# A gated ConvFFN on one core: from six token windows with copied leading columns to five windows of 512 and 384 columns with a carry table

## The chip, the core and the metric

The kernel runs on one core of a Trainium2 chip. The metric is the device time of one execution in microseconds (us), the median of several runs. The engines are TensorE (PE, matmul, with PEld for its weight loads), VectorE (DVE), ScalarE (ACT), GpSimd (POOL) and SyncE (SP, which here only issues transfers).

## The reference

One layer of a hybrid encoder over a prompt of 2048 tokens and 128 sample tokens (8 streams of 16), D_MODEL 1024: a mixer (a Mamba-2 group and a forgetting-attention group side by side), an output projection with a residual add, then the gated ConvFFN (D_FF 2816, convolution width 3) with a residual add, then a last RMSNorm. The change touches the FFN alone:

```python
def rmsnorm(x, g):
    y = xf * lax.rsqrt(jnp.mean(xf * xf, axis=-1, keepdims=True) + EPS)
    return y * g
def causal_dwconv(x, prev, w, b):          # w has 3 taps
    xp = jnp.concatenate([prev, x], axis=1)
    y = b
    for j in range(w.shape[0]):
        y = y + xp[:, j:j + L] * w[j]
    return y, xp[:, L:]
def conv_ffn(n, prev, w_up, cw, cb, w_down):
    u, new = causal_dwconv(n @ w_up, prev, cw, cb)
    g, v = u[..., :D_FF], u[..., D_FF:]
    return (silu(g) * v) @ w_down, new
# in the layer: x = h + conv_ffn(rmsnorm(h, norm2_g), ...); at the end rmsnorm(x, final_norm_g)
```

## The kernel before, in words

The 2176 tokens are 17 tiles of 128 rows, the sample tokens being the last tile. Everything up to the output projection writes h, a row of 1024 per token, to memory (`h_d`). The FFN then goes over the tokens in three parts (`FPARTS`); a part holds two windows of columns. All 198 weight blocks are read again for each part.

- **The weights.** `load_w` reads a block of 128x1024 on ACT's queue into one of 3 `raw` buffers; ACT casts it to a high half (L102) and POOL subtracts for the low half (L105, `split`), into one of 6 `wr` buffers. Every product is formed of three matmuls: high by high, high by low, low by high (L113 to L115, `mm3`).
- **The rows of a window.** `prep` makes `nT`, the normalised rows transposed: it loads a tile of h, ACT squares and sums it, POOL makes the inverse root (`rsq`, L108 and L109), DVE multiplies (L925), PE transposes eight blocks (`tp`, L929), ACT copies the high half and DVE subtracts the low one. In the parts after the first it loads the tile into the buffer `y`, which afterwards collects the result. A window's `nT` carries PAD2 = 2 leading columns, copied from the end of the window before it (L906), so that the convolution has its two preceding tokens: 386 columns for three tiles, and 258 for the last window (one prompt tile, the sample tile, the 2 columns).
- **Up.** For each of 22 feature blocks f (`NFF`) `up` makes a gate row block and a value row block: 24 matmuls each into one PSUM bank (`mm`, 5 banks), then ACT's eviction with the last tap and the bias (L951), DVE's two other taps, each reading the bank (L953), for the sample tile four more small ones and an add (L957, L959) and copies of the last columns to the output table `cs2` (L960, L961); then ACT's SiLU (L963), DVE's product of gate and value (L964) and its split into `ht` (L104, L105).
- **Down.** Two blocks f make a group (`GRP` = 2), eleven groups a part. `down` adds for each tile and each half of 512 columns six matmuls into one bank (`dn`, 3 banks; L975 to L977), which DVE adds to `y` (L978). With 6 tiles that is 72 matmuls a group, with 5 tiles 60.
- **Order.** A framework's scheduler places the instructions on the engines; PE's order is fixed by it, and a buffer that is not free makes the engine wait. Within a part a group's `down` matmuls stand among the next group's first up matmuls. At a change of part the first window of the next part is prepared after the last group's ups, and the second one in the first group of the next part. After the last group `finish` normalises each tile of `y` and writes it (L984 to L989).

## Time and profile before

| | |
|---|---|
| runs | 3183.7, 3184.08, 3178.56 us; median 3183.7 us |
| the profiled execution | 3180.02 us by its own time, of which the trace spans 3178.3 us; mean granted TensorE clock 0.978 |
| FFN in the trace | from the first up matmul at 1576.06 us to the last down matmul, which starts at 3170.47 us |
| busy in the span | PE 95%, DVE 58%, ACT 32%, POOL 28% |

Times in the trace are counted from the start of the span. A busy matmul in it overlaps the next one, so what one matmul costs in a stream is read from the distance of two starts, not from its duration.

### The profile page before, as it was taken

To read this page: it belongs to the slowest core of one execution; us is meant where nothing else is said; L and a number is where in the kernel's file an instruction comes from. 1 tells how busy PE (TensorE), PEld (TensorE's weight loads), DVE (VectorE), ACT (ScalarE), POOL (GpSimd) and SP (SyncE) were. 2 spreads that over 40 slices of the span, in tenths; PEclk is the share of its full clock that TensorE was granted. 3 is DMA by queue.
4 is the path that set the end of the run, shared out by engine and by line. 5 is a ranking of instruction groups with operands and counts; after the bars stand their busy time and mean duration, and the time that the engine had idled before them with its cause. 6 is when DMAs were issued, how large, how long until landed. Compare 5 with 4: busy or idle time off the path is not lost.

```text
span 3178.3 us, 45508 instructions
## 1 busy us (share of the span) xinstructions
PE 3035.1 (95%) x17808; PEld 2671.8 (84%) x17808; DVE 1829.3 (58%) x3325; ACT 1024.1 (32%) x1778; POOL 882.4 (28%) x574
## 2 busy tenths in 40 slices
PE   5998988899999998999999999999999999999999
PEld 5886866788778875677899999989999999999998
DVE  5355465757574655552355555566555556766666
ACT  3343332434333433322322222233222223322222
POOL 3223311332232223100232232323232232433332
PEclk9998988999999998999999999999999999999999
DMA  4856864576547545543621221233122222322221
GB/s 161 256 180 197 246 200 128 165 215 178 148 152 211 157 137 178 169 144 111 234 79 58 64 67 54 67 100 100 53 74 60 67 66 71 109 74 80 68 71 67
DMA packets 233854, 398.36 MB, mean 125 GB/s; under 512 B 62624, under 2 KB 118568, under 8 KB 233640
## 3 DMA queue, kind: packets, MB, share of 16 engines
q1 hardware_dynamic: 180072, 234.22, 23.9%
q10 hardware_dynamic: 53568, 161.24, 16.2%
q8 instruction: 140, 2.29, 0.3%
q14 instruction: 74, 0.61, 0.1%
HBM read 317.13 MB, written 78.25 MB: 124 GB/s over the span
## 4 chain that ended last, share of the span: by engine, by line
PE 84%; DMA 7%; DVE 4%; issue 2%; SPq 1%; POOL 1%; ACT 1%; ACTq 0%; POOLq 0%; DVEq 0%
PE mm L113 11%; PE mm L114 11%; PE mm L115 11%; PE pv L662 6%; PE dn L975 5%; PE dn L976 5%; PE dn L977 5%; PE mm L413 3%; PE mm L414 3%; PE mm L415 3%; PE dn L873 2%; PE mm L366 2%; PE dn L875 2%; PE mm L367 2%; PE dn L874 2%; PE mm L368 2%
## 5 line engine op out<-in xcount | busy, mean ns | idle before, releaser
L105 POOL TENSOR_TENSOR wr<-raw,wr 128x1024 fp32r<-128x1024 f32 x198 | 475.9, 2411 | 1032.8 <-ACT wr L102 985.8
L113 PE MATMUL mm<-nT,wr 128*128 128x386 f32 (+1 forms) x2112 | 696.5, 330 | 1.3 <-ACT wr L102 0.8
L114 PE MATMUL mm<-nT,wr 128*128 128x386 f32 (+1 forms) x2112 | 695.3, 329 | 0.1
L115 PE MATMUL mm<-nT,wr 128*128 128x386 f32 (+1 forms) x2112 | 694.5, 329 | 0.0
L953 DVE SCALAR_TENSOR_TENSOR ac<-mm,cw,ac 128x384 f32<-128x384 f32 (+1 forms) x528 | 301.7, 572 | 345.0 <-ACT ac L951 337.3
L951 ACT ACTIVATE ac<-mm,cw 128x384 f32<-128x384 f32 (+1 forms) x264 | 172.5, 653 | 785.9 <-PE mm L115 782.0
L978 DVE TENSOR_TENSOR y<-y,dn 128x512 f32<-128x512 f32 x374 | 255.3, 684 | 267.3 <-PE dn L977 264.5
L114 PEld LDWEIGHTS mm<-nT,wr 128*128 128x128 f32 x2112 | 399.4, 189 | 6.8 <-DVE nT L105 0.3
L113 PEld LDWEIGHTS mm<-nT,wr 128*128 128x128 f32 x2112 | 397.6, 188 | 7.7 <-ACT wr L102 1.1
L115 PEld LDWEIGHTS mm<-nT,wr 128*128 128x128 f32 x2112 | 398.0, 188 | 5.7
L105 POOL TENSOR_TENSOR cmw<-craw,cmw 128x1024 fp32r<-128x1024 f32 (+1 forms) x96 | 231.1, 2411 | 380.4 <-ACT cmw L102 295.9
L413 PE MATMUL mm<-nT,cmw 128*128 128x256 f32 (+2 forms) x1024 | 309.2, 302 | 1.6 <-DVE g_2k L300 1.6
L637 DVE TENSOR_REDUCE nm<-s 128x1 f32<-128x512 f32 (+2 forms) x320 | 192.5, 606 | 190.2 <-PE s L634 109.4
L414 PE MATMUL mm<-nT,cmw 128*128 128x256 f32 (+2 forms) x1024 | 298.6, 292 | 0.0
L415 PE MATMUL mm<-nT,cmw 128*128 128x256 f32 (+2 forms) x1024 | 297.9, 291 | 0.0
L662 PE MATMUL pv<-pr,v 128*128 128x512 f32 (+3 forms) x640 | 295.6, 552 | 2.2 <-POOL v L602 1.8
L975 PE MATMUL dn<-wr,ht 128*128 128x512 f32 x748 | 294.4, 394 | 2.8 <-DVE y L978 1.7
L976 PE MATMUL dn<-wr,ht 128*128 128x512 f32 x748 | 292.8, 391 | 0.0
L977 PE MATMUL dn<-wr,ht 128*128 128x512 f32 x748 | 290.1, 391 | 0.0
L102 ACT CAST wr<-raw 128x1024 fp32r<-128x1024 f32 x198 | 203.2, 1042 | 173.7 <-PE dn L977 161.5
L697 ACT ACTIVATE pr<-s 128x512 f32<-128x512 f32 (+1 forms) x320 | 169.7, 531 | 269.7 <-PE s L693 182.9
L634 PE MATMUL s<-ks,q 68*128 68x512 f32 (+2 forms) x320 | 201.4, 635 | 10.8 <-DMA q<-q_d 7.0
(287 smaller groups left out, 5194.9 us busy)
## 6 DMA issues: line engine op xcount, KB each, us to landing
raw<-in_w_up ACTq DMA_DIRECT2D x132, 512.0 KB
raw<-in_w_down ACTq DMA_DIRECT2D x66, 512.0 KB
craw<-in_w_cm ACTq DMA_DIRECT2D x64, 512.0 KB
k<-k_d SPq DMA_DIRECT2D x80, 256.0 KB
craw<-in_w_tm ACTq DMA_DIRECT2D x24, 512.0 KB
q_d<-qk SPq DMA_DIRECT2D x96, 128.0 KB
k_d<-qk SPq DMA_DIRECT2D x96, 128.0 KB
ks<-k_d SPq DMA_DIRECT2D x80, 136.0 KB
```

What stands on the lines that cost most here:

```text
L105: leng.tensor_sub(lo, src, hi.bitcast(F32))
L113: T.matmul(ps[:, :W], whi(k), wt[:, 0, k, :W], start=k == 0, stop=False)
L114: T.matmul(ps[:, :W], whi(k), wt[:, 1, k, :W], start=False, stop=False)
L115: T.matmul(ps[:, :W], wlo(k), wt[:, 0, k, :W], start=False, stop=k == n - 1)
L413: T.matmul(ps[:, :W], wc[:, 0, k, :], wk[:, 0], start=k == 0, stop=False)
L414: T.matmul(ps[:, :W], wc[:, 0, k, :], wk[:, 1], start=False, stop=False)
L415: T.matmul(ps[:, :W], wc[:, 1, k, :], wk[:, 0], start=False, stop=k == KT - 1)
L662: m = T.matmul(pv[:, of:512], vr[:, jj], pr[:, :512 - of], start=first, stop=last)
L953: V.scalar_tensor_tensor(ac[:, 0:n], ps[:, j:j + n], cw2[:, ct, j:j + 1], ac[:, 0:n], op0=ALU.mult, op1=ALU.add)
L975: T.matmul(ps, ht[:, 0, ts_], wd[:, 0, cc], start=x == 0, stop=False)
L976: T.matmul(ps, ht[:, 0, ts_], wd[:, 1, cc], start=False, stop=False)
L977: T.matmul(ps, ht[:, 1, ts_], wd[:, 0, cc], start=False, stop=x == len(g) - 1)
```

## The change

The windows become 512, then 256 and the sample tile (384 columns), 512, 384, 384; the parts have 7, 7 and 3 tiles, and the last part has a single window. The leading columns go. Instead `up` keeps the last two prompt columns of every row block in a table `cry` (a copy by DVE for each row block and window, into `cs2` in the last window), and in the four windows that do not begin at token 0 DVE adds each of the two earlier taps in two instructions: the inner columns from the PSUM bank, and the first two or the first column from `cry`. Both inputs of that second instruction lie in SBUF. Line numbers of the kernel after are one to ten lower; its taps are L943, the taps from the table L945, the copies L946, product L956, split L103 and L104, transposes L917, and down L967 to L970.

`prep` no longer shares `y`: it loads h into a buffer `nt` of its own (2 of them), squares in two halves, and `load_y` loads the `y` tiles after the first ups of each part. The two windows have an `nT` buffer each. The first window of the next part is prepared in the last group between the ups of its first and second window, the second one ahead of that group's `down`. `ht` has 3 buffers of 7 tiles, before 4 of 5 or 6. `finish` squares in halves.

```diff
-PAD2 = 2
 FPARTS = [
-    [(0, 384, False), (384, 768, False)],
-    [(768, 1152, False), (1152, 1536, False)],
-    [(1536, 1920, False), (1920, 2048, True)],
+    [(0, 512, False), (512, 768, True)],
+    [(768, 1280, False), (1280, 1664, False)],
+    [(1664, 2048, False)],
 ]
...
+    def load_y(c):
+        ys_[c] = yp.tile([P, D], F32, tag="y", name="y")
+        dA(ys_[c], h_d[c])
+
+    def prep(w, e):
+        W = win_width(w, 0)
+        wt = nTp.tile([P, 2, KT, (512, 384)[e]], F32R, tag=f"nT{e}", name="nT")
         for c in win_tiles(w):
...
-                src = yp.tile([P, D], F32, tag="y", name="y")
-                dA(src, h_d[c])
-                ys_[c] = src
-                S.activation(nt, src, AF.Square, accum_out=ss[:, 0:1])
+            dA(nt, h_d[c])
+            for a in range(2):
+                jk = tp.tile([P, 512], F32, tag="ac0", name="ac")
+                S.activation(jk, nt[:, a * 512:(a + 1) * 512], AF.Square, accum_out=ss[:, a:a + 1])
+            V.tensor_add(ss[:, 0:1], ss[:, 0:1], ss[:, 1:2])
             rsq(ss[:, 0:1], D)
...
             for j in range(2):
-                V.scalar_tensor_tensor(ac[:, 0:n], ps[:, j:j + n], cw2[:, ct, j:j + 1], ac[:, 0:n], op0=ALU.mult, op1=ALU.add)
+                d = 2 - j
+                wj = cw2[:, ct, j:j + 1]
+                V.scalar_tensor_tensor(ac[:, d:n], ps[:, 0:n - d], wj, ac[:, d:n], op0=ALU.mult, op1=ALU.add)
+                if w[0]:
+                    V.scalar_tensor_tensor(ac[:, 0:d], cry[:, ct, j:2], wj, ac[:, 0:d], op0=ALU.mult, op1=ALU.add)
+            V.tensor_copy((cs2 if w[1] == SEQ else cry)[:, ct, 0:2], ps[:, n - 2:n])
...
-                hts[f] = bp3.tile([P, 2, len(tiles) * P], F32R, tag="ht", name="ht", bufs=4)
+                hts[f] = bp3.tile([P, 2, 7 * P], F32R, tag="ht", name="ht", bufs=3)
...
-                if f0 == 0 and x > 0:
-                    prep(part[1])
-                    wins.append(nwin[-1])
-                for f in fs:
-                    one_up(f, 1)
+                if end and nxt:
+                    new.append(prep(nxt[0], 0))
+                if nw > 1:
+                    for f in fs:
+                        one_up(f, 1)
...
-            if f0 + GRP >= NFF and not last:
-                prep(FPARTS[x + 1][0])
+            if end and len(nxt) > 1:
+                new.append(prep(nxt[1], 1))
             down(g, tiles)
...
-    nTp = F.enter_context(tc.tile_pool(name="nT2", bufs=2, side="right", reuse_waits="tile"))
+    nTp = F.enter_context(tc.tile_pool(name="nT2", bufs=1, side="right", reuse_waits="tile"))
```

How the order on the engines changes is shown at three places. In the rows a name such as `ac_26725` is one buffer of the tile `ac`. First, DVE in the last part before: one block f of its 384-column window.

```order
L953 SCALAR_TENSOR_TENSOR ac_25736<-mm_25711,cw2_15371,ac_25736 128x384 x2
L953 SCALAR_TENSOR_TENSOR ac_25765<-mm_25740,cw2_15371,ac_25765 128x384 x2
L964 TENSOR_TENSOR ac_25736<-ac_25736,ac_25765 128x384
L104 CAST ht_25700<-ac_25736 128x384
L105 TENSOR_TENSOR ht_25700<-ac_25736,ht_25700 128x384
```

DVE in the last part of the kernel after: one block f of its only window, up to the cast.

```order
L943 SCALAR_TENSOR_TENSOR ac_26725<-mm_26700,cw2_15391,ac_26725 128x382
L945 SCALAR_TENSOR_TENSOR ac_26725<-cry_15402,cw2_15391,ac_26725 128x2
L943 SCALAR_TENSOR_TENSOR ac_26725<-mm_26700,cw2_15391,ac_26725 128x383
L945 SCALAR_TENSOR_TENSOR ac_26725<-cry_15402,cw2_15391,ac_26725 128x1
L946 COPY cs2_15401<-mm_26700 128x2
L943 SCALAR_TENSOR_TENSOR ac_26757<-mm_26732,cw2_15391,ac_26757 128x382
L945 SCALAR_TENSOR_TENSOR ac_26757<-cry_15402,cw2_15391,ac_26757 128x2
L943 SCALAR_TENSOR_TENSOR ac_26757<-mm_26732,cw2_15391,ac_26757 128x383
L945 SCALAR_TENSOR_TENSOR ac_26757<-cry_15402,cw2_15391,ac_26757 128x1
L946 COPY cs2_15401<-mm_26732 128x2
L956 TENSOR_TENSOR ac_26725<-ac_26725,ac_26757 128x384
L103 CAST ht_26689<-ac_26725 128x384
```

The two taps of a row block stood back to back, each in one instruction; now each is followed by one that reads the table, and a copy comes behind, also before the product of the two row blocks.

Second, PE in the last group of the first part, where the first rows of the next part are transposed. Before, they come behind the last up matmul of the group:

```order
L114 MATMUL mm_19402<-nT_15166,wr_19246 128x386
L115 MATMUL mm_19402<-nT_15166,wr_19246 128x386
L929 MATMUL tp_19455<-ident_71,nt_19447 128x128 x4
L929 MATMUL tp_19462<-ident_71,nt_19447 128x128 x4
L929 MATMUL tp_19477<-ident_71,nt_19469 128x128 x4
L929 MATMUL tp_19484<-ident_71,nt_19469 128x128 x4
L975 MATMUL dn_19513<-wr_19437,ht_19165 128x512
L976 MATMUL dn_19513<-wr_19437,ht_19165 128x512
```

After, they come behind the last up matmul of the first window and nine down matmuls of the first block f (`ht_19671`); the second window's ups (not shown) follow later.

```order
L967 MATMUL dn_20176<-wr_20076,ht_19671 128x512
L968 MATMUL dn_20176<-wr_20076,ht_19671 128x512
L969 MATMUL dn_20176<-wr_20076,ht_19671 128x512
L917 MATMUL tp_19833<-ident_71,nt_19822 128x128 x4
L917 MATMUL tp_19840<-ident_71,nt_19822 128x128 x4
L917 MATMUL tp_19858<-ident_71,nt_19847 128x128 x4
L917 MATMUL tp_19865<-ident_71,nt_19847 128x128 x4
L967 MATMUL dn_20160<-wr_20081,ht_19746 128x512
L968 MATMUL dn_20160<-wr_20081,ht_19746 128x512
...
L969 MATMUL dn_20176<-wr_20081,ht_19746 128x512
L917 MATMUL tp_19883<-ident_71,nt_19872 128x128 x4
```

Before, the first down matmuls of both blocks read tiles of the first window, whose rows of `ht` were made while the second window's ups ran. Now the down matmuls of the second block (`ht_19746`) read rows of the window that has just ended; they stand right behind the transposes of two tiles, and the third tile's transposes stand nine of them later.

Third, DVE at that place, before:

```order
L953 SCALAR_TENSOR_TENSOR ac_19398<-mm_19373,cw2_15371,ac_19398 128x384 x2
L953 SCALAR_TENSOR_TENSOR ac_19427<-mm_19402,cw2_15371,ac_19427 128x384 x2
L964 TENSOR_TENSOR ac_19398<-ac_19398,ac_19427 128x384
L105 TENSOR_TENSOR nT_19445<-tp_19455,nT_19445 128x4x128
L105 TENSOR_TENSOR nT_19445<-tp_19462,nT_19445 128x4x128
L104 CAST ht_19238<-ac_19398 128x384
L978 TENSOR_TENSOR y_15539<-y_15539,dn_19513 128x512
L105 TENSOR_TENSOR nT_19445<-tp_19477,nT_19445 128x4x128
L105 TENSOR_TENSOR ht_19238<-ac_19398,ht_19238 128x384
```

And after:

```order
L943 SCALAR_TENSOR_TENSOR ac_19812<-mm_19787,cw2_15391,ac_19812 128x510
L943 SCALAR_TENSOR_TENSOR ac_19812<-mm_19787,cw2_15391,ac_19812 128x511
L946 COPY cry_15402<-mm_19787 128x2
L104 TENSOR_TENSOR nT_19821<-tp_19833,nT_19821 128x4x128
L956 TENSOR_TENSOR ac_19782<-ac_19782,ac_19812 128x512
L104 TENSOR_TENSOR nT_19821<-tp_19840,nT_19821 128x4x128
L104 TENSOR_TENSOR nT_19821<-tp_19858,nT_19821 128x4x128
L104 TENSOR_TENSOR nT_19821<-tp_19865,nT_19821 128x4x128
L103 CAST ht_19746<-ac_19782 128x512
L104 TENSOR_TENSOR ht_19746<-ac_19782,ht_19746 128x512
```

The product and split for the last value row block made in that window were divided by two subtractions for `nT`; now by four, and the cast that the down matmuls of `ht_19746` read stands behind all four.

## Rows read from the trace of the kernel before

**Rows 1.** the page: busy time, share and instructions of each engine

```profile
PE 3035.1 (95%) x17808; PEld 2671.8 (84%) x17808; DVE 1829.3 (58%) x3325; ACT 1024.1 (32%) x1778; POOL 882.4 (28%) x574
```

**Rows 2.** busy time by stretch: a group of part 0, then of part 2

```profile
core 0: us, PE busy (x) PEld busy (x) DVE busy (x) ACT busy (x) POOL busy (x), PEclk, DMA share, GB/s
1687.73:1738.24 50.51, 50.51 (x266) 47.49 (x265) 27.93 (x41) 13.22 (x18) 14.35 (x8) 1.00 0.20 63
2842.48:2884.76 42.28, 42.28 (x255) 39.82 (x254) 28.13 (x59) 12.48 (x18) 14.63 (x8) 1.00 0.25 75
```

**Rows 3.** timeline of PE (start us, us, engine line op): three widths

```profile
1849.80 0.34 PE L113 MATMUL mm<-nT,wr 128*128 128x386 f32 x1
...
1859.70 0.34 PE L115 MATMUL mm<-nT,wr 128*128 128x386 f32 x1
...
2128.19 0.40 PE L975 MATMUL dn<-wr,ht 128*128 128x512 f32 x1
...
2130.02 0.39 PE L977 MATMUL dn<-wr,ht 128*128 128x512 f32 x1
...
2813.12 0.28 PE L113 MATMUL mm<-nT,wr 128*128 128x258 f32 x1
...
2815.88 0.29 PE L115 MATMUL mm<-nT,wr 128*128 128x258 f32 x1
```

**Rows 4.** groups by line and form, 1576:3179 (busy us, mean ns | idle before)

```profile
L105 POOL TENSOR_TENSOR wr<-raw,wr 128x1024 fp32r<-128x1024 f32 x198 | 475.9, 2411 | 1032.8 <-ACT wr L102 985.8 <-issue 38.9 <-PE dn L976 4.4
...
L953 DVE SCALAR_TENSOR_TENSOR ac<-mm,cw,ac 128x384 f32<-128x384 f32 x440 | 271.1, 617 | 337.4 <-ACT ac L951 331.2
L978 DVE TENSOR_TENSOR y<-y,dn 128x512 f32<-128x512 f32 x374 | 255.3, 684 | 267.3 <-PE dn L977 264.5
...
L964 DVE TENSOR_TENSOR ac<-ac 128x384 f32<-128x384 f32 x110 | 173.4, 1577 | 3.7
L951 ACT ACTIVATE ac<-mm,cw 128x384 f32<-128x384 f32 x220 | 147.7, 671 | 706.4 <-PE mm L115 702.5 <-POOL wr L105 3.7
...
L105 DVE TENSOR_TENSOR ht<-ac,ht 128x384 fp32r<-128x384 f32 x110 | 63.2, 574 | 3.0
...
L959 DVE TENSOR_TENSOR ac<-ac,sc 128x16 f32<-128x16 f32 x44 | 51.7, 1176 | 0.0
L104 DVE CAST ht<-ac 128x384 fp32r<-128x384 f32 x110 | 39.3, 357 | 2.9
...
L929 PE MATMUL tp<-ident,nt 128*128 128x128 f32 x88 | 11.2, 273 | 1.8 <-DVE nt L925 1.8
...
L960 DVE COPY cs<-mm 128x2 f32<-128x2 f32 x44 | 6.6, 149 | 0.0
```

**Rows 5.** busy time by stretch: the two changes of part (columns as above)

```profile
2091.84:2253.75 161.91, 158.12 (x842) 147.12 (x841) 104.70 (x153) 58.36 (x90) 53.43 (x43) 1.00 0.32 98
2657.85:2800.21 142.36, 140.94 (x815) 131.22 (x814) 102.61 (x184) 52.74 (x82) 50.52 (x37) 1.00 0.30 97
```

**Rows 6.** waits of PE in 1576:3179 (us in total, times, longest)

```profile
PE tp L929 <- DVE nt L925: 1.8, 3, 1.3
```

**Rows 7.** timeline of SP's queue, ACT and DVE around one early tile

```profile
1553.00 0.37 SPq L913 DMA_DIRECT2D nt<-h_d  x1
...
1557.46 0.63 ACT L916 ACTIVATE ac<-nt 128x512 f32<-128x512 f32 x1 [2.52 <-DMA nt<-h_d]
...
1560.89 1.28 DVE L925 SCALAR_TENSOR_TENSOR nt<-nt,ss,g2B 128x1024 f32<-128x1024 f32 x1 [0.71 <-POOL ss L109]
```

**Rows 8.** timeline of DVE and POOL in part 2

```profile
2806.45 2.40 POOL L105 TENSOR_TENSOR wr<-raw,wr 128x1024 fp32r<-128x1024 f32 x1 [0.23 <-ACT wr L102]
...
2807.59 1.30 DVE L959 TENSOR_TENSOR ac<-ac,sc 128x16 f32<-128x16 f32 x1
```

**Rows 9.** timeline of PE: an idle time ahead of the FFN

```profile
402.38 0.77 PE L634 MATMUL s<-ks,q 68*128 68x512 f32 x1 [4.29 <-DMA q<-q_d]
```

**Rows 10.** busy time by stretch around that idle time

```profile
402.00:408.00 6.00, 5.62 (x27) 3.08 (x28) 2.46 (x8) 0.54 (x3) 0.00 (x0) 0.50 0.42 149
```

70 lines of the change are left out of this document (28 added, 42 removed).

## The prediction

> **What bounds the kernel now.** The page's line of engines comes first: PE is busy 95% of the span, DVE 58% [rows 1]. The FFN is tighter still. One group of part 0, taken as a stretch, is 50.51 us long and PE is busy in all of it; one of part 2 is 42.28 us and again full, at a granted clock of 1.00, while DVE works 27.93 and 28.13 us and POOL 14.35 and 14.63 [rows 2]. So in the body of a part the time is PE's matmuls and nothing else. What one costs is read in the timeline from start to start [rows 3]: 386 columns 9.90 us over 56 steps, 176.8 ns; 258 columns 2.76 over 23, 120.0 ns; 512 columns (down) 1.83 over 8, 228.8 ns. Check: 192 x 0.1768 + 72 x 0.2288 = 50.4 us, the group's 50.51; 96 x (0.1768 + 0.1200) + 60 x 0.2288 = 42.2 us, the other's 42.28.
>
> Only at the changes of part does PE lose time. The stretch 2091.84 to 2253.75 is three groups plus 48 transposes; 88 of them are 11.2 us of busy time, 0.127 each [rows 4], and since busy time counts the overlap too I take 0.11 from start to start, an estimate: 161.91 - 3 x 50.51 - 5.3 = 5.1 us lost. The other holds one group of 50.51, two of 42.28 and 40 transposes: 142.36 - 135.07 - 4.4 = 2.9 us [rows 2, 5]. Together 8.0 us. The waits that PE shows by name are small: for the transposes three, 1.8 us in all [rows 6].
>
> **The change part by part**, against the profiled execution's own 3180.0 us.
>
> *Up matmuls: -22 us.* A window takes 24 matmuls for each of 44 row blocks (22 f, gate and value), 1056. Before, one matmul of each of the six windows is 5 x 176.8 + 120.0 = 1004.0 ns; after there are two of 512 and three of 384. For 384 I take the 386 row less two columns at (176.8 - 120.0)/128 = 0.444 ns: 175.9. For 512 there is a down row of equal width, 228.8; a row in up form is not in the trace. After: 457.6 + 527.7 = 985.3, saving 18.7 x 1.056 = 19.8 us. The period of whole groups gives more: with 228 for 512 the 386 come to 177.6 and 258 to 120.3, saving 23.4. I take 22. Bounds: the straight line through 386 and 258 gives 232.7 for 512, saving 11.5 us; 384 columns at the slope alone, without any fixed price, 170.5, would save 37. The down matmuls, 2244, do not change, nor the 198 weight blocks, nor the 136 transposes.
>
> *Changes of part: +6 us (-3 to +12).* At the first one three waits are new, from the order shown. (1) The down matmuls of `ht_19746` need the cast of a row block whose last matmul ends at t = 0. Nine downs (2.06 us) and 16 transposes (1.76) cover 3.8 us. The chain is ACT's eviction (0.67 at 384 columns, so about 0.8 at 512), two taps at 0.617 x 512/384 = 0.82, a copy, one subtraction for `nT` that starts at about 3.1 us, after the first transposes and ACT's copy of them (all subtractions and the product of 512 elements at 0.574 x 512/384 = 0.77), the product, three more subtractions, the cast (0.48): 3.1 + 5 x 0.77 + 0.48 = 7.4 us [rows 4]. PE waits 3.6 us. (2) Only two `nt` buffers exist, so the third tile's load starts when the first tile's transposes end, at 2.9 us. From a load's issue to the end of DVE's multiplication one early tile took 1553.00 to 1562.17 = 9.2 us [rows 7]: ready at 12.1, while PE, after wait (1) and nine downs, is there at 9.5: 2.6 us more. (3) The last tile of the second window has 12 + 9 downs and 8 transposes ahead, 5.7 us against 9.2: 3.5 us. The second change of part has (1) with 384 columns, about 2, and (3) shortened by it, 1.5. Sum 13.2 (3.6 + 2.6 + 3.5 + 2 + 1.5); I add 1 us for the clock. An idle PE costs more than its wait: after 4.29 us of idle time earlier in the kernel the granted clock was 0.50, so 1.2 instead of 2.4 GHz, for 6 us [rows 9, 10], some 3 us of work. What a wait of 3 us does to it no row shows; between nothing and these 3 us I take a third. 14.2 against the 8.0 lost before. Lower bound: if loads land early enough, (2) and (3) vanish and 5 us are left, -3. Upper: waits half longer and one stretch at half clock, +12.
>
> *DVE in the last part: +6.5 us (0 to +16, at the extreme +35).* A group there is 96 x 0.176 + 36 x 0.2288 = 25.1 us of PE, and one window a group leaves DVE fewer matmuls to hide behind. DVE needs 8 taps at 0.617, 4 copies and 8 table taps at 0.149 (no row has a table tap; it lies between the two-column copy, 0.149, and the 128x16 add, 1.176, whose inputs both lie in SBUF, and I count the excess below), two products and two subtractions at 0.574, two casts at 0.357, six adds at 0.684: 4.9 + 1.8 + 2.3 + 0.7 + 4.1 = 13.8 us [rows 4]. That fits. But an operation with both inputs in SBUF waits for POOL here: the product at 384 columns has a mean of 1577 ns where the subtraction of the same shape has 574, and the 128x16 add 1176 [rows 4]; in the timeline that add starts while POOL subtracts and takes 1.30 us [rows 8]. In a group of part 2 this costs DVE 2 x 1.0 + 4 x 1.03 = 6.1 us of POOL's 14.6, 42%. In the last part ten operations a group are of that kind, and POOL does its 6 x 2.41 = 14.5 us in 25.1. At 42% DVE is at 19.9 us, at 100% at 28.3, above PE's 25.1: +3.2 x 11 = +35. The value taken is nearer the first: a product or a table tap can be held by each POOL instruction only once. What is left is latency: the last up of a group has 9 downs and 29 matmuls, 7.2 us, until PE needs its rows of `ht`; the chain is 0.67 + 1.23 + 0.45 + 0.57 + 0.36 = 3.3 us alone, and with one or two holds of POOL (2.4 each) and two adds ahead (1.4) 7.1 to 9.5. About 0.6 us a group, 11 groups.
>
> The Trainium skill (SBUF — State Buffer, Who interferes with whom) says that a DVE instruction with two SBUF inputs contends with a GpSimd instruction that reads SBUF, and that the second to issue is blocked, not slowed. The trace agrees, by the 1577 and 1176 ns.
>
> *The same table taps in parts 0 and 1: +1 (0 to +5).* There DVE has 58 us a group (192 matmuls of 0.202 on average, 84 of 0.2288) for work of 33 to 47 us (its 27.93 a group of 6 tiles and two windows, scaled to 7, and all of POOL's 14.35 on top); only the changes of part feel it.
>
> *The end: +1.5.* Behind the last up matmul nine downs (2.06 us) stand ahead of those that read its `ht`, ready 3.3 to 3.9 us later: +1.8. Squares in halves give back 0.3.
>
> *Edits at nothing.* The copies of leading columns, the squares by halves and the wider `y` loads hide beside 50 us of matmuls a group; if the loads of `y` were late, their first use is 38 us after the first ups, far more than 9.2. Three `ht` buffers instead of four: the one that is reused has been read by `down` two row blocks earlier; if not, each group waits for a chain of about 3.5 us. Weights are read as often, but in the last part in 25.1 us a group instead of 42.28, which takes the DMA share of 0.25 [rows 2] to about 0.42; POOL's halves stay ahead by six `wr` buffers; without that a group loses up to 2.4 us.
>
> Sum: -22 + 6 + 6.5 + 1 + 1.5 = -7: 3173.0 of the execution's own time. The median of the runs is 3.7 us above the profiled one and the fastest run 1.5 below it; I forecast 3174.
>
> **The rivals.**
>
> *Full gain.* The scheduler's waits are covered: loads land before they are needed, POOL and DVE miss each other. For it: DVE's share in the last part is about 80% at the 42% above. Against it: the order, where nine downs stand against a chain of 9.2 us. -22 - 3 + 0 + 1 + 1.5 = -22.5, so 3158.5.
>
> *No change.* Waits at the changes of part and in the last part eat the gain: +12, +10, +1 and +1.5 against -22, +2.5 or 3183.5. Or up matmuls follow the straight line of the two up widths (11.5 saved instead of 22): 3184.5 with the other terms as above. For it: both up widths are in the trace and 512 in up form is not; against it, both group periods come out with 228.8 for a down matmul of that width.
>
> The Trainium skill (TensorE: Matmul & The Clock Gate, Back-to-back issue gap) gives columns/2.4 + 2.5 ns for a matmul alone, so hardly a fixed price. By it the change would save only 7.9 us and the sum would be about 3188; the same section calls it too high at 512 in a stream, where it has 131 ns, and the trace shows neither: 176.8 for 386 columns against 163.3, 228.8 for 512.
>
> *Slower.* DVE becomes the bound in the last part: table taps behind POOL hold DVE, `ht` comes late, and each group of 25.1 us grows. It decides from 1.5 us a group beyond my 0.6 (16 us over eleven groups, to 3190); with all of POOL's time it is +35 instead of +6.5, 3202.5; I put it at 3196. For it: ten operations of the kind that [rows 8] shows and POOL at 58%; against it: at 42% DVE has 5 us spare in each group.
>
> **How the numbers follow.** Chances: forecast (3166 to 3181) 0.48, full gain 0.12, no change (by waits, 0.13, by the line, 0.10) 0.23, slower 0.17. The measurement tells 0.2%, 6.4 us, from no change: faster below 3177.3, slower above 3190.1. The forecast lies below for three quarters (0.36, the full gain adds 0.12, and 0.06 of the no-change cases fall below): 0.54; slower 0.17; the same 0.29. The range reaches down to the full gain and up to the start of the slower case, leaving out half of the one and most of the other: 3158 to 3192; the likeliest one's own is 3166 to 3181.
>
> **What would show it.** In the profile after: up at 512 from start to start 228 and at 384 about 176; PE full in the groups of the first two parts, in 58.1 us; groups of 25 to 26 us in the last part; waits of PE named tp behind L913 and dn behind the cast L103 at two places, 13 us together; L945 with a mean above 0.5 us. Wrong would be: 512 at 232 or more, groups of the last part above 27.5 us, or changes of part that lose less than 6 or more than 20 us.

## The result and the profile after

The kernel after takes 3195.54 us (median of 7 runs, 3186.15 to 3196.97), the kernel before 3178.56 us in the runs beside it (7 runs, 3176.26 to 3184.08): a ratio of 1.0045, 95% interval 1.0031 to 1.0058. The change makes the kernel slower, by about 14 us by that ratio (17 between the medians); the forecast was 3174, its range 3158 to 3192.

The profiled execution of after is one of 3195.54 us, with a span of 3193.8 us, 15.5 more than before. The first up matmul starts at 1580.37 us instead of 1576.06. Of these 4.3 us, 3.6 are there at the last matmul of attention's value product (1501.59 instead of 1498.03 us), ahead of the change. From that matmul to the first up it is 78.0 us before and 78.8 in every other kernel profiled here, while the first up itself starts anywhere between 1568 and 1583 us: what comes ahead of the value product differs from one profiled execution to the next, whatever the edit. So the comparison goes from the first up matmul to the end of the last down matmul, 1594.6 us before and 1604.6 after, and stretch by stretch.

First the groups, as stretches of after (the columns are those of [rows 2]): one of the first part, one of the last, and the stretch behind a long wait, of which more below.

```profile
core 0: us, PE busy (x) PEld busy (x) DVE busy (x) ACT busy (x) POOL busy (x), PEclk, DMA share, GB/s
1747.39:1805.78 58.39, 58.39 (x278) 50.68 (x276) 39.63 (x75) 13.49 (x18) 14.59 (x7) 1.00 0.16 54
3000.84:3025.93 25.09, 25.09 (x133) 23.62 (x132) 22.71 (x32) 9.36 (x13) 15.04 (x6) 1.00 0.36 126
2200.00:2211.00 11.00, 8.94 (x34) 7.47 (x35) 7.89 (x13) 5.03 (x12) 2.45 (x4) 0.69 0.38 123
```

PE is full in both kinds of group, as in [rows 2], although DVE is busy for 22.71 of 25.09 us in the last part. Eleven groups of each part make 11 x (58.38 + 58.37 + 25.09) = 1560.2 us, against 11 x (50.51 + 50.51 + 42.27) = 1576.2 before: 16 us less. What a matmul costs is again read from start to start, in the timeline of PE of after:

```profile
1773.58 0.34 PE L112 MATMUL mm<-nT,wr 128*128 128x384 f32 x1
...
1781.85 0.34 PE L114 MATMUL mm<-nT,wr 128*128 128x384 f32 x1
1782.03 0.40 PE L112 MATMUL mm<-nT,wr 128*128 128x512 f32 x1
...
1786.69 0.40 PE L114 MATMUL mm<-nT,wr 128*128 128x512 f32 x1
```

384 columns take 8.27 us over 47 steps, 176.0 ns, and 512 columns 4.66 over 20, 233 ns.

Between the groups PE waits more than before. Its waits in the FFN of after, which answer to [rows 6]:

```profile
PE dn L967 <- DVE ht L103: 8.4, 4, 2.8
PE dn L967 <- DVE y L970: 5.4, 5, 1.4
PE tp L917 <- DVE nt L913: 4.2, 3, 2.4
PE mm L114 <- POOL wr L104: 2.4, 3, 1.6
PE tp L917 <- DVE ss L911: 2.1, 1, 2.1
...
```

To place this, the FFN is cut into stretches, and the loss of a stretch is its length less its matmuls at their price in a full group (up 177.6 ns for 386 columns, 120.3 for 258, 233.0 for 512, 176.0 for 384, down 227.8, a transpose 109). These prices are fitted to the groups' lengths, with one price for a down matmul in all kernels; [rows 3] have 176.8 for 386 columns and 228.8 for a down. "Start" goes to the third group, a change from the first up of a part's last group to the fourth group of the next part, "end" from the last group to the last down matmul; the stretches between lose at most 0.6 us in any kernel here. In the first change of after, for example, all of the loss lies ahead of the next part's second group: 2156.14 to 2297.14 is 141.0 us and holds 192 ups of 512, 192 of 384, 168 downs and 56 transposes, 122.9 us; 18.1 are lost. The last column is the time from there to the end of the span.

| us | FFN | start | first change | second change | end | behind it |
|---|---|---|---|---|---|---|
| before | 1594.6 | 0.9 | 5.2 | 2.8 | 0.0 | 7.6 |
| after | 1604.6 | 6.9 | 18.1 | 8.1 | 2.2 | 8.9 |

So 16 us are gained and 26 lost again: 6.0 at the start, 12.9 and 5.3 at the changes, 2.2 at the end. With 4.3 ahead of the FFN and 1.3 behind it this is the 15.5 us of the spans, to within the rounding and the few tenths of the stretches between.

At the first change the rows of after show each wait that the prediction named. PE, and the clock behind it:

```profile
2200.34 0.57 PE L967 MATMUL dn<-wr,ht 128*128 128x512 f32 x1 [2.82 <-DVE ht L103]
2200.70 0.63 PE L968 MATMUL dn<-wr,ht 128*128 128x512 f32 x1
2201.13 0.63 PE L967 MATMUL dn<-wr,ht 128*128 128x512 f32 x1
...
2205.04 1.07 PE L917 MATMUL tp<-ident,nt 128*128 128x128 f32 x8 [0.79 <-DVE nt L913]
...
2232.79 1.07 PE L917 MATMUL tp<-ident,nt 128*128 128x128 f32 x8 [2.11 <-DVE ss L911]
2236.63 0.50 PE L967 MATMUL dn<-wr,ht 128*128 128x512 f32 x1 [1.38 <-DVE y L970]
...
2245.15 1.94 PE L917 MATMUL tp<-ident,nt 128*128 128x128 f32 x8 [2.44 <-DVE nt L913]
```

After the 2.82 us of waiting for the cast the down matmuls follow at 0.43 us instead of 0.23: the granted clock of that stretch is 0.69 (above). It is 0.56 from 2200.3 to 2203 and from 2207 to 2210.6 us, and 0.87 between the two, where PE waits twice more. The wait at 2232.79 and the one at 2236.63 were not foreseen. The second one has its cause in these rows of DVE and POOL at that place:

```profile
2233.23 0.47 DVE L943 SCALAR_TENSOR_TENSOR ac<-mm,cw,ac 128x254 f32<-128x254 f32 x1
2233.62 2.36 DVE L945 SCALAR_TENSOR_TENSOR ac<-cry,cw,ac 128x2 f32<-128x2 f32 x1
2235.90 0.67 DVE L970 TENSOR_TENSOR y<-y,dn 128x512 f32<-128x512 f32 x1
```

```profile
2233.59 2.37 POOL L104 TENSOR_TENSOR wr<-raw,wr 128x1024 fp32r<-128x1024 f32 x1
```

A table tap of two columns stands on DVE for as long as POOL subtracts, and the add to y behind it, which frees a PSUM bank for the next down matmul, comes some 2.1 us late (the same tap takes 0.21 us where POOL is idle). Over the FFN of after the groups by form say how often:

```profile
L945 DVE SCALAR_TENSOR_TENSOR ac<-cry,cw,ac 128x1 f32<-128x1 f32 x176 | 222.6, 1265 | 0.0
...
L945 DVE SCALAR_TENSOR_TENSOR ac<-cry,cw,ac 128x2 f32<-128x2 f32 x176 | 91.7, 521 | 0.0
...
L104 DVE TENSOR_TENSOR ht<-ac,ht 128x384 fp32r<-128x384 f32 x66 | 51.7, 783 | 1.8
...
L103 DVE CAST ht<-ac 128x384 fp32r<-128x384 f32 x66 | 40.3, 610 | 1.8
L956 DVE TENSOR_TENSOR ac<-ac 128x384 f32<-128x384 f32 x66 | 38.5, 583 | 0.8
```

The 352 taps hold DVE for 314 us. The product of 384 columns, held to 1577 ns in [rows 4], now takes 583 (the one of 512 columns 1039): the taps ahead of it take its place behind POOL. The cast and the subtraction that follow have become longer (357 to 610, 574 to 783). In the trace, 204 of the 352 taps overlap no subtraction of POOL, and they take 0.20 to 0.22 us; the 148 that do overlap one take 1.83 on average.

At the second change PE waits for the cast of ht twice, 1.89 and 2.37 us. Ahead of the second of these casts, finish's two products stand on DVE beside two subtractions, and a tap of two columns follows that is held for 2.30 us more:

```profile
2914.19 5.65 DVE L983 SCALAR_TENSOR_TENSOR y<-y,ss,gfB 128x512 f32<-128x512 f32 x2
...
2920.56 2.30 DVE L945 SCALAR_TENSOR_TENSOR ac<-cry,cw,ac 128x2 f32<-128x2 f32 x1
```

```profile
2914.09 5.21 POOL L104 TENSOR_TENSOR wr<-raw,wr 128x1024 fp32r<-128x1024 f32 x2
```

At the start, two rows of after: SP issues nine loads of y in a row, and the cast of a weight block waits 9.34 us for transfers.

```profile
1583.90 5.57 SPq L897 DMA_DIRECT2D y<-h_d  x9
...
1590.96 1.05 ACT L101 CAST wr<-raw 128x1024 fp32r<-128x1024 f32 x1 [9.34 <-DMA y<-h_d]
```

Before, SP issued the nine loads of y between 1507 and 1515 us, ahead of the last output projections:

```profile
1507.21 1.14 SPq L1017 DMA_DIRECT2D y<-h_d  x2
...
1509.85 2.18 SPq L1017 DMA_DIRECT2D y<-h_d  x4
1512.90 1.95 SPq L921 DMA_DIRECT2D y<-h_d  x3
```

The change opens the pool of y only when the output projection's buffers are given back.

### The profile page after: what moved, and what is told of

It reads as the page before. It is cut to its first block, busy times and chain, and to the rows that moved or that the text cites. A ratio compares the mean times of both kernels' runs of the same rounds, so it can differ in the third digit from the quotient of the medians.

```text
span 3193.8 us, 43834 instructions
## 1 busy us (share of the span) xinstructions
PE 3024.8 (95%) x16752; PEld 2566.9 (80%) x16752; DVE 2013.4 (63%) x3721; ACT 1004.8 (31%) x1768; POOL 891.5 (28%) x574
## 5 line engine op out<-in xcount | busy, mean ns | idle before, releaser
L104 POOL TENSOR_TENSOR wr<-raw,wr 128x1024 fp32r<-128x1024 f32 x198 | 485.7, 2461 | 1029.2 <-ACT wr L101 993.7
L114 PE MATMUL mm<-nT,wr 128*128 128x384 f32 (+1 forms) x1760 | 635.6, 361 | 2.4 <-POOL wr L104 2.4
L112 PE MATMUL mm<-nT,wr 128*128 128x384 f32 (+1 forms) x1760 | 635.9, 361 | 0.3 <-ACT wr L101 0.3
L113 PE MATMUL mm<-nT,wr 128*128 128x384 f32 (+1 forms) x1760 | 635.0, 361 | 0.0
L970 DVE TENSOR_TENSOR y<-y,dn 128x512 f32<-128x512 f32 x374 | 252.5, 682 | 246.0 <-PE dn L969 245.8
L943 DVE SCALAR_TENSOR_TENSOR ac<-mm,cw,ac 128x511 f32<-128x511 f32 (+5 forms) x440 | 281.9, 641 | 190.8 <-ACT ac L938 183.8
L114 PEld LDWEIGHTS mm<-nT,wr 128*128 128x128 f32 x1760 | 331.0, 188 | 35.7 <-POOL wr L104 3.6
L112 PEld LDWEIGHTS mm<-nT,wr 128*128 128x128 f32 x1760 | 331.3, 188 | 33.9 <-ACT wr L101 0.7
L113 PEld LDWEIGHTS mm<-nT,wr 128*128 128x128 f32 x1760 | 331.2, 188 | 32.8
L938 ACT ACTIVATE ac<-mm,cw 128x512 f32<-128x512 f32 (+1 forms) x220 | 156.0, 710 | 604.8 <-PE mm L114 545.0
L104 POOL TENSOR_TENSOR cmw<-craw,cmw 128x1024 fp32r<-128x1024 f32 (+1 forms) x96 | 231.1, 2411 | 379.4 <-ACT cmw L101 300.8
L945 DVE SCALAR_TENSOR_TENSOR ac<-cry,cw,ac 128x2 f32<-128x2 f32 x352 | 314.3, 893 | 0.0
L967 PE MATMUL dn<-wr,ht 128*128 128x512 f32 x748 | 295.3, 395 | 13.8 <-DVE ht L103 8.4
L101 ACT CAST wr<-raw 128x1024 fp32r<-128x1024 f32 x198 | 203.3, 1042 | 194.6 <-PE dn L969 176.0
```

What stands on the lines that cost most here:

```text
L104: leng.tensor_sub(lo, src, hi.bitcast(F32))
L112: T.matmul(ps[:, :W], whi(k), wt[:, 0, k, :W], start=k == 0, stop=False)
L113: T.matmul(ps[:, :W], whi(k), wt[:, 1, k, :W], start=False, stop=False)
L114: T.matmul(ps[:, :W], wlo(k), wt[:, 0, k, :W], start=False, stop=k == n - 1)
L945: V.scalar_tensor_tensor(ac[:, 0:d], cry[:, ct, j:2], wj, ac[:, 0:d], op0=ALU.mult, op1=ALU.add)
L967: T.matmul(ps, ht[:, 0, ts_], wd[:, 0, cc], start=x == 0, stop=False)
```

## The experiments

Theory: 26 us are lost at the start and at the changes of part, by (a) a burst of y loads ahead of weight loads, (b) two `nt` buffers that make transposes late, (c) table taps that POOL holds where DVE's queue is what PE waits for; and the gain of the matmuls is smaller than forecast since 512 columns cost 233 ns in an up matmul. Rival: DVE, held by POOL, slows the groups throughout. All readings are of one profiled execution each, in the stretches above; the ratio to the kernel before, measured beside it on the same chip, stands with them. How far the two can be trusted is seen from e5_pitch, which does the work of after: start, first and second change lose 5.5, 19.0 and 8.3 us there against 6.9, 18.1 and 8.1, yet its ratio is 1.0018 against 1.0045, and in its trace the last value product comes 8 us earlier. So the ratios of two kernels differ here by 0.3% with no cause in the FFN, and none of the single edits e1 to e4 and e8 has a ratio below e5's. What an edit is worth is read from the stretches, and there a difference of 1 us shows nothing.

**The y loads held back** (e1_ygate; 7 y buffers, since the two that are free would load for the next part).

```diff
-YB = 9
+YB = 7
...
+        if ht is not None:
+            V.tensor_copy(ys_[c][:, 0:2], ht[:, 0, 0:2].bitcast(F32))
         dA(ys_[c], h_d[c])
...
-                            load_y(c)
+                            load_y(c, hts[fs[n // 4]] if x == 0 else None)
```

> The kernel after, with 7 instead of 9 y buffers, and the y loads of the first part held back by a two-column copy out of ht (the first four tiles until the first block's ht is there, the other three until the second's). Theory A, that the 6.9 us lost in the first two groups of part 0 (0.9 before) come from weight loads queued behind a burst of nine y loads: the wait of the weight cast at 1591 us and PE's waits there go, the loss of the first two groups falls from 6.9 to 1 to 2 us, FFN from first up to last down from 1604.3 to about 1599 us, the rest of the stretches unchanged. Rival B, that the wider matmuls need the first weights sooner: the loss stays at 5 to 7 us, FFN about 1604.

Start 2.4, first change 16.8, second 10.0, end 2.2, FFN 1600.6; ratio 1.0028 (1.0013 to 1.0042). The wait of 9.34 us is gone (the weight cast there waits 3.3 for its load), theory (a) holds for 4.5 of the 6 us. The second change got 1.9 us worse without an edit there; where POOL's subtractions fall beside DVE can have shifted, but that is not shown.

**Four nt buffers** (e2_nt4; the third and fourth tile of a window from another pool, the squares into a tile of their own, 7 y buffers).

```diff
-            nt = tp.tile([P, D], F32, tag="nt", name="nt")
...
+            tq = more[0] if more and n % 4 > 1 else tp
+            nt = tq.tile([P, D], F32, tag="nt", name="nt")
...
-                jk = tp.tile([P, 512], F32, tag="ac0", name="ac")
+                jk = more[0].tile([P, 512], F32, tag="jk", name="jk", bufs=1) if more else tp.tile([P, 512], F32, tag="ac0", name="ac")
```

> The kernel after, with 7 y buffers, two more nt buffers for the third and fourth tile of a window, and a tile of its own for the unused squares, which stood in ac0. Theory A, that the two nt buffers (and the squares that wait for ac0) make the transposes late at the changes of part: the waits of PE on nt and ss there (6.3 us in 4) go, the loss at the first change falls from 18.1 to about 9 us, at the second from 8.2 to about 6; FFN about 1594 us (with two y loads fewer at the start another 1 to 2 less). Rival B, DVE's queue is what is late there (nt multiplications behind held table taps): the waits only change their name, the loss stays above 14, FFN above 1600.

Start 8.7, first change 11.1, second 10.5, FFN 1602.0; ratio 1.0021 (1.0009 to 1.0032). The waits for transposes shrink (one of 2.0 us is left), 7 us are won at the first change, but the downs there now wait 4.6 us for y, and the second change is worse. At the start PE waits 3.6 us at once for POOL: with free buffers the scheduler squares the next part's first tiles there, and POOL makes their roots ahead of the first weights. Neither theory fits whole; (b) is a part.

**Without the table taps** (e3_notap; the first columns of four windows lack their earlier taps).

```diff
-                if w[0]:
-                    V.scalar_tensor_tensor(ac[:, 0:d], cry[:, ct, j:2], wj, ac[:, 0:d], op0=ALU.mult, op1=ALU.add)
```

> The kernel after without the 352 table taps (L945): the first two columns of four windows lack their earlier taps; the copies into the table stay. Theory A, that the taps cost time only at the changes of part, where DVE's queue is late anyway: groups stay at 58.4 and 25.1 us, the loss at the first change falls by 2 to 4 us (two of its waits on y stand behind taps held 2.3 us by POOL), FFN about 1600 us. Rival B, that DVE held by POOL is the cause of the slower kernel: FFN falls by 10 us or more, to 1594 or less.

Start 5.4, first change 15.2, second 7.8, FFN 1600.6; ratio 1.0025 (1.0014 to 1.0036). The groups are 58.4 to 58.5 and 25.1 us long, no shorter than with the taps. So 314 us of DVE time cost 4 us, all outside the full groups; the rival, that DVE held by POOL slows the groups throughout, falls. What the held taps cost at the changes isn't settled by this run: PE's waits there only change (for the cast of ht 4.1 instead of 2.8 us at the first change, for y 1.1 instead of 2.5).

**The preparations at their old places** (e4_prepback).

```diff
-                if end and nxt:
-                    new.append(prep(nxt[0], 0))
+                if f0 == 0 and x > 0 and nw > 1:
+                    wins.append(prep(part[1], 1))
...
-            if end and len(nxt) > 1:
-                new.append(prep(nxt[1], 1))
+            if end and nxt:
+                new.append(prep(nxt[0], 0))
```

> The kernel after with the preparations at their old places: the first window of the next part behind the last group's ups of both windows, the second window in the first group of the next part. Theory A, that the new place puts the cast for the second block's down matmuls behind four subtractions for nT and the third tile's load behind nine downs: the wait on the cast (2.9 us and the half clock behind it) goes, the loss at the first change falls from 18.1 to 8 to 10 us and at the second from 8.2 to 4 to 6; FFN about 1592 us. Rival B, the two nt buffers alone cause the loss wherever the preparation stands: the loss at the first change stays above 13, FFN above 1598.

First change 12.7, second 9.6, FFN 1600.3; ratio 1.0024 (1.0011 to 1.0037). The place is worth 5 us at the first change, 1.5 of which the second gives back, and it doesn't remove the loss: one wait for the cast of ht, now of 3.7 us, stands elsewhere. The run doesn't decide between its two theories: 12.7 is neither 8 to 10 nor above 13.

**Another pitch of nT** (e5_pitch).

```diff
-        wt = nTp.tile([P, 2, KT, (512, 384)[e]], F32R, tag=f"nT{e}", name="nT")
+        wt = nTp.tile([P, 2, KT, (520, 392)[e]], F32R, tag=f"nT{e}", name="nT")
```

> The kernel after with rows of nT that are 8 columns longer than the windows (520 and 392), so that the moving rows of the up matmuls start at other addresses; the work is the same. Theory A, that an up matmul of 512 columns costs what the straight line through 258 and 386 columns gives (232.7 ns), whatever the pitch: start to start stays at a median of 231 to 233 ns, a group of the first two parts at 58.4 us. Rival B, that the pitch of 2048 bytes makes it slower than a down matmul of 512 columns: 227 to 229 ns, a group at 57.9 us, FFN 10 us shorter (1594).

The mean spacing of the 512-column ups is 232.3 ns, 233.0 in after, the groups are 58.37 and 25.06 us long, the FFN 1603.8; ratio 1.0018 (1.0007 to 1.0030). The pitch is not it.

**Held loads, four buffers and a whole-tile square together** (e6_all).

```diff
-        for e in range(2):
-            cc = slice(e * 512, (e + 1) * 512)
-            S.activation(nt[:, cc], y[:, cc], AF.Square, accum_out=ss[:, e:e + 1])
-        V.tensor_add(ss[:, 0:1], ss[:, 0:1], ss[:, 1:2])
+        S.activation(nt, y, AF.Square, accum_out=ss[:, 0:1])
```

> Together: y loads of the first part held back (e1), two more nt buffers and a tile for the squares (e2), and finish squaring a whole tile at once as before the change. Theory A, losses at different places add: start 2.4, first change 10 to 11, second 9 to 10, end 2.2, sum about 25 us against 35 after and 9 before; FFN 1594 to 1596, as long as before the change, and the tail half a us shorter. Rival B, the waits move from one place to the next: sum above 29, FFN above 1598.

Start 9.0, first change 16.8, second 10.9, FFN 1608.2; ratio 1.0046 (1.0028 to 1.0064). The sum of the single effects was wrong: the waits moved. At the start PE again waits 3.6 us at once for POOL, as in e2_nt4, where the next part's squares stand among the first weights. Only finish's square is clear: the time behind the last down matmul is 7.9 us instead of 8.3 to 8.9.

**The scaling of finish on ACT** (e8_finact; leaves out the product with final_norm_g in the first two parts).

```diff
-            V.scalar_tensor_tensor(y[:, cc], y[:, cc], ss[:, 0:1], gfB[:, cc], op0=ALU.mult, op1=ALU.mult)
+            if wins:
+                S.activation(y[:, cc], y[:, cc], AF.Identity, scale=ss[:, 0:1])
+            else:
+                V.scalar_tensor_tensor(y[:, cc], y[:, cc], ss[:, 0:1], gfB[:, cc], op0=ALU.mult, op1=ALU.mult)
```

> The kernel after, in which finish of the first two parts scales y on ACT by the inverse root alone; the product with final_norm_g is left out there. Theory A, that at the second change finish's DVE products (two SBUF inputs, 5.65 us for two at 2914 us) are held by POOL's weight subtractions and make ht late for the first down matmuls of the short part: the wait of 2.5 us at 2921 us goes, the loss at the second change falls from 8.1 to 5 to 6 us; at the first, where POOL has fewer weights to do, by 0 to 1. Rival B, those down matmuls wait for the table taps or the up matmuls anyway: the second change stays at 7 to 8.5 us.

First change 16.1, second 7.1, FFN 1601.9; ratio 1.0031 (1.0012 to 1.0050). At the second change, where after waits 2.37 us for the cast of ht, this kernel waits 1.18 and a little later 0.72. That finish's product holds DVE is worth about 1 us there, no more than after and e5_pitch differ by at the first change; it is not the cause.

**No taps and four buffers** (e9_notap_nt4: e1, e2 and e3 together).

> e1 and e2 together, without the 352 table taps (the first columns of four windows lack their earlier taps). Theory A, that what is left of the first change's loss with four nt buffers (11 us) comes from DVE operations held by POOL at a moment when DVE is late: the first change falls to 6 to 8 us, the second to 7 to 9. Rival B, that the order of the instructions alone makes the loss: the first change stays at 10 to 11.

Start 6.4, first change 7.7, second 0.1, FFN 1586.4; ratio 0.9993 (0.9979 to 1.0006). Against e6_all, which has the taps (and finish's whole-tile square), 22 us less. Against e3_notap, which has two buffers and doesn't hold the y loads, the first change loses 7.7 instead of 15.2 us and the second 0.1 instead of 7.8. Together the two edits do what neither did alone, so the next kernels carry the taps without the operation that POOL holds.

**The carried taps in the eviction's bias** (e10_bias). DVE writes bias plus earlier taps of the two columns into the table, reading the PSUM bank, and ACT evicts each of the two columns with its table entry as bias.

```diff
-            S.activation(ac[:, :W], ps[:, :W], AF.Identity, scale=cw2[:, ct, 2:3], bias=cw2[:, ct, 3:4])
+            lo = 2 if w[0] else 0
+            S.activation(ac[:, lo:W], ps[:, lo:W], AF.Identity, scale=cw2[:, ct, 2:3], bias=cw2[:, ct, 3:4])
+            for a in range(lo):
+                S.activation(ac[:, a:a + 1], ps[:, a:a + 1], AF.Identity, scale=cw2[:, ct, 2:3], bias=cry[:, ct, a:a + 1])
...
+                V.tensor_scalar(cry[:, ct, 0:2], ps[:, n - 2:n], cw2[:, ct, 0:1], cw2[:, ct, 3:4], op0=ALU.mult, op1=ALU.add)
+                V.scalar_tensor_tensor(cry[:, ct, 0:1], ps[:, n - 1:n], cw2[:, ct, 1:2], cry[:, ct, 0:1], op0=ALU.mult, op1=ALU.add)
```

> The kernel after, with the table taps carried otherwise: DVE writes into the table what the first two columns need (bias and earlier taps, from the PSUM bank, no operation with two SBUF inputs), and ACT evicts the first two columns by themselves with it as their bias. Theory A, the table taps cost time as DVE operations with two SBUF inputs beside POOL: as without taps (e3), start 5 to 6, first change 15, second 8, FFN about 1600 to 1601. Rival B, what helped in e3 was only that DVE had less to do: here DVE has as many instructions on the window's end and ACT more, FFN stays at 1603 to 1605.

Start 3.6, first change 10.9, second 9.0, FFN 1595.7; ratio 1.0016 (1.0000 to 1.0031). It wins 8.9 us against after, more than leaving the 352 taps out (4.0), though DVE has only 176 small instructions fewer (396 for the table instead of 352 taps and 220 copies) and ACT 352 more. That speaks for the kind of operation and against their number. But e3, which has none of the operations, should then win as much; why this kernel wins more than e3 is open, and so is how much of the 8.9 us is due to the taps. With the y loads held in both kernels the same edit, with finish's whole-tile square, is worth 5.0 us (e1_ygate to e12_nt2, below).

**All together, and two kernels that take a part of it back** (e11_best; e12_nt2 takes back the buffers, with the squares in ac0 and the preparation free to move as in after; e13_tapback takes back the taps alone, which come from the table again). All three hold the y loads and square whole tiles in finish. In e11_best and e13_tapback the preparation is held behind the group before:

```diff
-                    new.append(prep(nxt[0], 0))
+                    with tc.issue_after(past[-1]):
+                        new.append(prep(nxt[0], 0))
```

> Together: the carried taps through the eviction's bias (e10), y loads of the first part held back (e1), four nt buffers and a tile for the squares (e2), the preparation at a change issued no earlier than the last group's neighbour, and finish squaring a whole tile at once. Theory A, the two causes at the changes (two nt buffers, and DVE operations held by POOL) must both be gone: start 2 to 3, first change 4 to 8, second 0 to 2, end 2, FFN 1579 to 1585, 10 to 15 us shorter than before the change, and faster than it by 0.3 to 0.5%. Rival B, it stays at the sum of the single effects (35 less 4, 4 and 3): FFN about 1594, the same as before the change.

> The previous one with the two nt buffers of the change and squares in ac0. Theory A, two nt buffers alone keep the transposes late: first change 13 to 16, second 5 to 8, FFN about 1592. Rival B, once DVE isn't held, the loads are in time: first change below 9, FFN about 1585.

> The best one (four nt buffers, held y loads, held preparation) with the change's own taps from the table back, and nothing else. Theory A, the taps held by POOL: first change 10 to 14, second 8 to 11, FFN 1591 to 1597. Rival B, in the earlier run with four nt buffers the loss came from the preparation that had moved to the start: first change 5 to 8, second 0 to 3, FFN as the best one.

| us | taps | nt buffers | FFN | start | first change | second change | end | behind it |
|---|---|---|---|---|---|---|---|---|
| e6_all | table | 4, preparation free | 1608.2 | 9.0 | 16.8 | 10.9 | 2.2 | 7.9 |
| e1_ygate | table | 2 | 1600.6 | 2.4 | 16.8 | 10.0 | 2.2 | 8.3 |
| e12_nt2 | bias | 2 | 1595.6 | 0.9 | 16.5 | 5.9 | 2.4 | 7.9 |
| e13_tapback | table | 4, preparation held | 1593.4 | 2.3 | 9.0 | 10.7 | 2.2 | 7.9 |
| e11_best | bias | 4, preparation held | 1576.7 | 0.7 | 3.4 | 0.4 | 2.4 | 7.9 |

e11_best takes 3165.71 us beside 3182.62 of the kernel before: a ratio of 0.9948 (0.9928 to 0.9968), faster by about 17 us. e12_nt2 is at 1.0022 (1.0007 to 1.0037), e13_tapback at 0.9990 (0.9976 to 1.0005). With two buffers and the free preparation 16.5 and 5.9 us are lost at the two changes, with the table's taps 9.0 and 10.7, without either 3.4 and 0.4. From e13_tapback to e11_best only the taps differ, and they are worth 16.7 us.

The held preparation is a third cause beside these two. From e6_all to e13_tapback it is all that differs, and the FFN becomes 14.8 us shorter: 6.7 at the start and 7.8 at the first change. PE's first wait for a low half, in e6_all and then in e13_tapback (window 1560 to 1690):

```profile
PE mm L114 <- POOL wr L104: 3.6, 1, 3.6
```

```profile
PE mm L114 <- POOL wr L104: 0.4, 1, 0.4
```

e12_nt2 lacks the buffers, the squares' own tile and the hold together, so its 18.9 us against e11_best aren't shared out between them; e9_notap_nt4, which has the buffers, no taps and no hold, loses 6.4 at the start and 7.7 at the first change where e11_best loses 0.7 and 3.4.

PE's waits in the FFN of e13_tapback and then, in a fence of its own, of e11_best:

```profile
PE dn L970 <- DVE y L973: 6.6, 5, 3.0
PE dn L970 <- DVE ht L103: 6.0, 2, 4.6
PE tp L920 <- DVE ac L955: 2.1, 1, 2.1
...
```

```profile
PE dn L975 <- DVE y L978: 1.9, 2, 1.6
PE dn L975 <- DVE ht L103: 1.5, 1, 1.5
PE tp L920 <- DVE cs L961: 0.7, 1, 0.7
...
```

The 4.6 us of e13_tapback are one wait, in the first group of the last part. DVE, POOL and PE there, from the timeline:

```profile
2904.12 0.21 DVE L948 SCALAR_TENSOR_TENSOR ac<-cry,cw,ac 128x2 f32<-128x2 f32 x1
...
2904.90 2.08 DVE L948 SCALAR_TENSOR_TENSOR ac<-cry,cw,ac 128x1 f32<-128x1 f32 x1
...
2909.56 2.02 DVE L948 SCALAR_TENSOR_TENSOR ac<-cry,cw,ac 128x1 f32<-128x1 f32 x1
...
2913.42 0.35 DVE L103 CAST ht<-ac 128x384 fp32r<-128x384 f32 x1
```

```profile
2904.57 2.40 POOL L104 TENSOR_TENSOR wr<-raw,wr 128x1024 fp32r<-128x1024 f32 x1 [1.30 <-ACT wr L101]
...
2909.23 2.34 POOL L104 TENSOR_TENSOR wr<-raw,wr 128x1024 fp32r<-128x1024 f32 x1 [1.76 <-ACT wr L101]
```

```profile
2908.85 0.34 PE L114 MATMUL mm<-nT,wr 128*128 128x384 f32 x1
2913.83 0.80 PE L970 MATMUL dn<-wr,ht 128*128 128x512 f32 x1 [4.64 <-DVE ht L103]
```

Two taps of one column, each as long as what is left of a subtraction on POOL, take 4.1 us instead of 0.4 ahead of the cast. By an estimate from these rows the cast would start at about 2909.7 us without the hold, half a microsecond behind the end of the last up matmul, so the hold is most of the wait; the rows don't show what else would then stand ahead of it.

## Why the prediction was wrong

The forecast sum was -7 us, the profiled spans differ by +15.5. Term by term, in us:

| term | forecast | measured |
|---|---|---|
| up matmuls | -22 | -15 |
| changes of part | +6 | +18 |
| DVE in the last part | +6.5 | 0 |
| taps in parts 0 and 1, felt at the changes | +1 | in the +18 above; 0 in the groups |
| end | +1.5 | +3.5 |
| start (edits at nothing) | 0 | +6 |
| ahead of the value product | 0 | +3.6, in this execution |

What is left of the difference is rounding and the stretches between. The step that failed is the cost of the changes of part: it was the sum of three waits, each worked out by itself, with 1 us for the clock, and the taps that POOL holds up in DVE's queue, which only the changes were to feel, stood beside it with +1. Together that is 7 us more than before, and 18 were measured; with the held taps, the two buffers and the free preparation gone together (e11_best) the changes lose 3.8 us, less than before. Beside it the loads of y, put at nothing, cost 6 at the start, and the saving of the matmuls was taken 7 too large. Two of the prediction's three signs of being wrong are there: 512 columns at 232 ns or more (233), and changes that lose more than 20 us (26). The third, groups of the last part above 27.5 us, is not.

- **Up matmuls, -22 us: mis-sized.** The stretches give 16 us, of which 0.9 are eight transposes that moved ahead of the FFN, so 15. By mean spacings in full groups the ups alone give 12 (177.0 and 120.2 ns before, 233.0 and 175.9 after) and the rest is in down matmuls about 1.5 ns cheaper than before; the split is not settled. The 384 columns came out as forecast (176.0); 512 columns cost 233 ns, not the 228 of a down matmul of that width. The bound that I set by the straight line through 258 and 386 columns, 232.7, was the value; the rival built on it gave 11.5 us with 386 at 176.8. Taking the price from a row of the same width but another kind of matmul was the error, worth 2112 x 5 ns = 10.6 us against the sum by the groups' periods (23.4), of which 384 columns at 176.0 instead of the 176.7 in that sum gave 2.2 back.
- **Changes of part, +6 us: mechanism right, size wrong.** 26.1 us lost against 8.0 before, +18. The three waits of the first change were there, and each a little smaller than forecast: for the cast 2.8 (forecast 3.6), for the third tile 0.8 and for the fourth 0.9 (2.6), for the last tile 2.4 (3.5). Missing were the wait of 2.1 us for squares that need a free ac0, the two on y (2.5; the first right behind a held tap, the second behind subtractions for `nT` in the same late queue), and the half clock, for which a third of 3 us was put in: nine downs at 0.43 us and seven ups at 0.32 are 2.8 us more than at full clock, in one of the places. At the second change the forecast had 3.5 us; 8.1 were lost, 4.3 of it in two waits for the cast, the second behind finish's products and a tap that POOL held.
- **DVE in the last part, +6.5 us: wrong as placed.** The groups are 25.09 us long, as PE's matmuls give (25.1), with DVE busy 22.7 where 19.9 were forecast. The rival that made DVE the bound there fell too, so that the kernel came out slower is not for that rival's reason. Its mechanism, though, is what cost time elsewhere: the groups are as long with the taps as without them (e3_notap), while at a change of part, where ht and y are needed at once, a held tap shows up in PE's waits. Leaving the taps out is worth 4.0 us (e3), carrying them through the bias 8.9 (e10_bias), and with four nt buffers and the preparation held (e13_tapback to e11_best) 16.7. The contrast that the forecast drew, 1577 ns for the product against 574 for the subtraction of the same shape, was no contrast in kind: that subtraction reads two SBUF tiles too (`ac` and `ht`). With taps ahead of both, the product falls to 583 ns and the subtraction rises to 783, which points to the place beside POOL, not to the kind, as what told the two apart.
- **Edits at nothing: wrong at the start.** "If the loads of y were late" asked about y alone. They were not late; the weights behind them were. 6 us, 4.5 of which came back by holding the loads (e1_ygate), and all of it with the taps in the bias as well (e12_nt2, e11_best).
- **The end, +1.5 us: too small.** It is 2.2 in the matmuls and 1.3 behind them. Squares in halves cost 0.4 to 1 us there (8.3 to 8.9 in the kernels with them, 7.9 in those without) instead of giving 0.3.
- **The chances.** Slower had 0.17, given to DVE as the bound of the full groups, where nothing was lost. The way it came, by the changes of part and the start, had no rival of its own; the nearest was no change by waits (0.13), which allowed the changes +12.

Open is why a 512-column up matmul takes 5 ns more than a down matmul of the same width; the pitch of its moving rows is excluded (e5_pitch).

## What to carry to other kernels

Price a stream by rows of the same kind of instruction, and when two widths of it are there, trust their line before a row of another kind. Small DVE operations with both inputs in SBUF, beside a busy GpSimd, cost nothing here in a steady stretch and microseconds where the pipeline is refilled; reading one operand from PSUM and handing the addition to ScalarE's bias took them out. At a change of stage remove the causes together before judging one of them: of the 26.1 us lost at the two changes e13_tapback and e12_nt2, which each take a part back, still lose 19.7 and 22.4, and e11_best, with taps, buffers and preparation all changed, 3.8. Before trusting a ratio of some tenths of a per cent, look in the trace for a stretch that the edit can't reach and see whether it moved as much.

## What the runs showed of the hardware

- A DVE operation on one column per partition can take 2.3 us: the table taps had a mean of 1265 ns (one column) and 521 (two), beside GpSimd's subtractions of 2.4 us. The 204 of after that overlap no such subtraction take 0.20 to 0.22 us, the 148 that overlap one 1.83 on average.
- Not only operations with two SBUF inputs are held. The cast of 384 columns, one input in SBUF, went from a mean of 357 to 610 ns; of all 110 casts of ht in after ten overlap a subtraction of GpSimd and take 2.46 us on average, the others 0.39. The Trainium skill (SBUF — State Buffer, Who interferes with whom) counts casts among the operations that can take the ports shared with GpSimd, and the trace agrees, by the 2.46 against 0.39 us.
- A wait of 2.82 us on PE was followed by matmuls at half speed (0.43 us for 512 columns) at a granted clock of 0.56 from 2200.3 to 2203 us, and two more waits of 0.79 and 0.93 by another such stretch (0.32 us for 384 columns, granted 0.56 from 2207 to 2210.6).
- In a stream, up matmuls follow 5.5 ns + 0.444 ns a column from 258 to 512 columns to within 1 ns (120.3, 176.0, 177.6 and 233.0 ns at 258, 384, 386 and 512), down matmuls of 512 columns take 227.8.
